# The last layer's expert outputs: added to rows in SBUF by one-hot products on TensorE, instead of accumulated in HBM by indirect DMA

## The chip, the cores and the metric

The kernel runs on one core of a Trainium2 chip. The metric is the device time of one execution in microseconds. The engines are TensorE (PE in the rows, its weight loads PEld), VectorE (DVE), ScalarE (ACT), GpSimd (POOL) and SyncE (SP). A name with q behind it (ACTq, SPq, POOLq) is the part of an engine that issues DMAs. The DMA engines, 16 for the core, carry out what all queues issue.

## The reference

Two layers run over 512 latent tokens and 256 context tokens of width 1024. Each layer has four token mixers, an output projection with a residual, and then expert-choice routing: every one of 16 experts takes the 64 latent tokens (and 32 context tokens, in the first layer only) with the highest scores, runs a SwiGLU network on them, and adds its result to their rows. The last layer's latent rows are the output.

```python
def _ec_ffn(h, w_router, w_gate, w_up, w_down):
    cap = max(1, EC_FACTOR * N // N_EXPERTS)
    aff = jax.nn.softmax((h @ w_router).astype(jnp.float32), axis=-1)
    g, idx = lax.top_k(aff.transpose(0, 2, 1), cap)
    xe = h[bidx, idx]
    hid = (jax.nn.silu(jnp.einsum('becd,edf->becf', xe, w_gate))
           * jnp.einsum('becd,edf->becf', xe, w_up))
    ye = jnp.einsum('becf,efd->becd', hid, w_down) * g[..., None]
    return jnp.zeros_like(h).at[bidx, idx].add(ye)
...
x = x + gt1 * x_mix
h2 = _modulate(_rmsnorm(x, g_ffn[l]), sh2, sc2)
x = x + gt2 * _ec_ffn(h2, w_router[l], w_gate_e[l], w_up_e[l], w_down_e[l])
```

A token may be among the 64 of several experts, or of none; its row then gets several additions, or none.

## The kernel before

Each layer has a stage of mixers (`mixers`), a stage `out_and_route` and a stage `experts`. All matrices are f32.

`out_and_route` finishes the output projection and adds it to the residual rows `x_res` (`resid`, lines 1229 to 1231). `turn` transposes the rows for the router and, once a tile of 128 rows is complete, stores it: in the last layer to `out` itself, on ACT's queue (line 1416). `norm` (lines 1270 to 1274) makes h2, mostly in place, over `x_res`, and ACT's queue stores it to the HBM rows `h2s`. `top` finds the 64 tokens of each expert by eight rounds on VectorE and ends with the indices `idx4` (line 1330), `idx2` (line 1344) and the weights `gval2`.

`experts` then runs expert after expert. POOL gathers the expert's rows of h2 from `h2s` (`gather`, line 1485, an indirect DMA), VectorE transposes them (`turn`, line 1494), TensorE multiplies by w_gate and w_up (`gu`, line 1512, four blocks of weights), ACT and VectorE make `hid` (lines 1521 to 1523), TensorE multiplies by w_down (`down`, line 1545, two blocks), VectorE scales the result to `y_e` (line 1547, 64 tokens in two halves of 512 columns on 128 partitions), and POOL adds it to `out` in HBM by an indirect DMA that accumulates (`add`, line 1526). The half of the partitions with the first 512 columns of the tokens is 0 to 63, the other 64 to 127. TensorE's order is: gate-up blocks A of expert e, w_down of e−1, blocks B of e.

The weights come by SP's queue in loads of 2816 KB, called `w_ex` (`ex_load`, line 1445; the first ones, line 1440, from a copy `w_head` in other order). At most two are in flight (QUEUED = 2). A load's place in SBUF is a block of 22,528 bytes of each partition. A planner (`place`) lays out the whole arena of 183,296 bytes from the life of every tile; beside what else lives in this stage of the last layer, eight blocks fit, and a load waits until the matmuls that read the block's former weights are done. Loads are asked for in the order w_down(e), B(e+1), A(e+2). The planner tries orders of placement drawn from a seed for each part of the program (`SEEDS`), and the schedule of the mixers follows from the plan.

PSUM tiles of the kinds `dn_ps` and `sum_ps` come from one pool (`MM`) of three buffers; the gate-up products use others (`SC`).

Of the kernel before, what the change touches and what calls it, by code (L numbers as in the profile page):

```python
# [17 lines left out]
OP = mybir.AluOpType  # L18
AX = mybir.AxisListType

D = 1024
T = 512
TC = 256
NT = T + TC
L = 2
EPS = 1e-6
E_N = 16
# [26 lines left out]


ARENA = 183296
SEEDS = 48, 0, 1, 0


def lifetimes(instructions, asked):  # L60
# [26 lines left out]
def place_part(lives, room, part, seed, done, tries=400):  # L87

    rnd = random.Random(seed)
    order = sorted(part, key=lambda n: (lives[n][1] - lives[n][0] < 2000, lives[n][0]))  # L90
    for _ in range(tries):
        offs = dict(done)
        for n in order:
            o = fit(lives, room, offs, n)
            if o is None:
                break
            offs[n] = o
        else:
            return offs
        order.remove(n)  # L100
        with_n = [i for i, m in enumerate(order) if m in offs and lives[m][0] <= lives[n][1] and lives[m][1] >= lives[n][0]]
        order.insert(rnd.choice(with_n) if seed and with_n else 0, n)
# [21 lines left out]
class Block:  # L124
# [1043 lines left out]
    def out_and_route(self, l, xs_src, x_dst, ctx_dst):  # L1168
# [9 lines left out]
        next(prelude)  # L1178
        order = cx + lat
        N = len(order)  # L1180
        xr = [self.Q([3, 1024], "x_res") for _ in range(2)]
        rows_x = [xr[n // 3][:, n % 3] for n in range(N)]
        for n, i in enumerate(order):
            self.load_tokens(rows_x[n], xs_src[0 if i < 4 else 1], i, (nc.sync, nc.sync))
        early = [lambda p=p: self.ex_load(l, 0, p, 0) for p in "AAAABBBB"]
        early += [lambda e=e, p=p: self.ex_load(l, e, p, 1) for e, p in HEAD[2:] for _ in range(2)]
        for _ in range((2, 4)[l]):
            early.pop(0)()

# [46 lines left out]
        def turn(n, z):  # L1236
            if z == 0:
                xTs[n] = self.E4([8, 128], "x2T")
            ps = self.MM("x2_tp")
            for k in range(4):  # L1240
                c = 128 * (4 * z + k)
                nc.tensor.transpose(ps[:, 128 * k:128 * k + 128], rows_x[n][:, c:c + 128], self.ident)
            nc.scalar.copy(xTs[n][:, 4 * z:4 * z + 4], ps.rearrange("p (k t) -> p k t", k=4))
            if z:
                i = order[n]
                self.store_tokens(x_dst if i < 4 else ctx_dst, rows_x[n], i, nc.scalar)

# [16 lines left out]
        def norm(n):  # L1264

            i = order[n]
            x, r = rows_x[n], rows[0 if i < 4 else 1]
            h = x if n < N - 2 else self.E4([1024], "h2")
            if n < N - 1:
                nc.vector.scalar_tensor_tensor(h, x, rs[:, i:i + 1], r[:, 2], op0=OP.mult, op1=OP.mult)  # L1270
            else:
                nc.scalar.mul(h, x, rs[:, i:i + 1])
                nc.gpsimd.tensor_mul(h, h, r[:, 2])
            nc.gpsimd.tensor_add(h, h, r[:, 1])
            return lambda *keep: self.store_tokens(self.h2s[0 if i < 4 else 1], h, i, nc.scalar, *keep)
# [2 lines left out]
        self.gval = self.K([3, 16], "gval")  # L1278
        self.idx2 = self.K([16], "idx2", I32)
        self.gval2 = self.K([16], "gval2")  # L1280
        self.groups = [0, 0] + ([] if last else [1])

        def top(m, w):
# [49 lines left out]
            if m == 0:  # L1333
# [8 lines left out]
                nc.vector.tensor_mul(d2[:, 3], d2[:, 3], d2[:, 2])  # L1342
                nc.vector.tensor_add(d2[:, 4], d2[:, 3], d2[:, 0])
                nc.vector.tensor_scalar(self.idx2, d2[:, 4], 0.5, self.misc[:, 6:7], op0=OP.mult, op1=OP.add)
                nc.vector.tensor_tensor(self.gval2, p2[:, 0, 1], d2[:, 1], op=OP.max)

        pick = self.E3([2, 2, 128], "pick", p=64)
# [114 lines left out]
    def experts(self, l, x_rows, tops, tail, early):  # L1462


        nc, io = self.nc, self.io
        G = len(self.groups)
        every = list(range(G))
        hv = [h.rearrange("n (j c) -> (n j) c", j=4) for h in self.h2s]
        xv = [x.rearrange("n (j c) -> (n j) c", j=4) for x in x_rows]
        x2 = x_rows[0].rearrange("n (h c) -> (n h) c", h=2)  # L1470
        wgt = self.wgt

        def load(e, part):
            if e < E_N:
                for _ in range(2 // 1):
                    self.ex_load(l, e, part, 1)

        XG, XT, PG, HID, HT, BK = {}, {}, {}, {}, {}, {}

# [49 lines left out]
        def down(e):  # L1529
# [15 lines left out]
                    nc.tensor.matmul(ps[32 * q:32 * q + 32], HT[e][:, g, k], self.w_dn(e, k, 512 * h, 512 * h + 512),  # L1545
                                     start=(k == 0), stop=(k == 10))
            nc.vector.scalar_tensor_tensor(y[:, 0:512], ps, self.gval2[:, e:e + 1], self.gt2[0], op0=OP.mult, op1=OP.mult)  # L1547
            add(x2, self.idx2[:, e:e + 1], y[:, 0:512])
            del HT[e], HID[e], XT[e], wgt[e]


        if G == 3:
# [16 lines left out]
        gather(1, every)  # L1569
        gu(0, 0, 4, [0, 1])  # L1570
        self.marks.append(len(self.asked))
        load(1, "B")
        gu(0, 4, 8, [0, 1])
        load(2, "A")
        hid(0, [0, 1])
        turn(1, every)
        for e in range(2, 4):
            gather(e, every)
        for e in range(1, E_N):
            gu(e, 0, 4, every)  # L1580
            load(e, "D")
            down(e - 1)
            load(e + 1, "B")
            if e + 1 < E_N:
                turn(e + 1, every)
            gu(e, 4, 8, every)
            load(e + 2, "A")
            hid(e, every)
            if e + 3 < E_N:
                gather(e + 3, every)  # L1590
        down(E_N - 1)

    def run(self):
# [130 lines left out]
def layout(inputs):  # L1724
# [43 lines left out]
    fw = np.zeros((L, 128, 3, 256), np.float32)  # L1768
    fw[:, :, 0], fw[:, 1:, 1], fw[:, ::32, 2] = w[:, 0:128], w[:, :128:-1], w[:, 128:129]
    io["fnet_w"] = fw  # L1770
    io["w_out"] = f("w_out")
    io["w_router"] = f("w_router").reshape(L, 8, 128, 16).transpose(0, 2, 1, 3)

# [44 lines left out]
```

## Time and profile before

| what | value |
| --- | --- |
| three runs | 2737.04, 2738.1, 2740.97 us |
| median | 2738.1 us |
| the profiled execution, its own time | 2742.23 us |
| its span | 2740.4 us |
| granted clock of TensorE, mean over the span | 0.957 |
| TensorE busy | 2429.4 us, 89% |
| VectorE busy | 983.3 us, 36% |
| stage of the mixers, layer 1 | 0 to 985 us, with what stands ahead |
| stages of routing and experts, layer 1 | 985 to 1475 us |
| stage of the mixers, layer 2 | 1475 to 2020 us |
| routing, layer 2 | 2020 to 2092 us |
| experts, layer 2 | 2092 to 2741 us |

The bounds of the stages are read off the timeline and are rough. A row of a window gives the stretch and its length, then the busy time of PE, PEld, DVE, ACT and POOL with the number of instructions, then the granted clock (1.00 is the 2.4 GHz level), the mean busy share of the DMA engines and their GB/s. In a row of a timeline stand the start, the length, the engine and line, the operation with the tiles out<-in, how many instructions the row holds, and in brackets how long the engine was idle ahead of it and what ended that. Two records stand for one f32 matmul. A row of a DMA queue gives packets, MB and the time of its packets as a share of the 16 engines.

### The profile page before, as it was taken

The page shows a single profiled execution, that of the slowest core. Times are in us where ns is not written, and L with a number is a line of the kernel's source. Part 1 is how long each engine was busy: PE and PEld are TensorE (multiplying, and loading weights), DVE is VectorE, ACT ScalarE, POOL GpSimd, SP SyncE. Part 2 cuts the span into 40 slices and gives each one's busy share as a digit, 9 for nine tenths or more (in the row PEclk, how much of TensorE's full clock was granted, in tenths as well). Part 3 has the DMA queues.
Part 4 walks back from the last instruction along what each step waited for, and adds up shares of the span by engine and source line. Part 5 has one row for each costly group of instructions (what it writes and reads, how often), then busy time and mean ns, then how long its engine had stood idle before and what let it go on. Part 6 is the DMA issues. An engine that isn't in the chain of part 4 may idle for free. (4 is left out here: it accounts for less than half of the span.)

```text
span 2740.4 us, 48684 instructions
## 1 busy us (share of the span) xinstructions
PE 2429.4 (89%) x21446; PEld 1679.8 (61%) x21446; DVE 983.3 (36%) x1986; ACT 577.4 (21%) x1094; POOL 474.3 (17%) x347
## 2 busy tenths in 40 slices
PE   7989889999969999999997799999974977777776
PEld 5778889999845555677774677877862422222222
DVE  5666547643251111111112765477432110110101
ACT  4324445433310000000001424344320000000000
POOL 1352332211240111111001211011121111010100
PEclk9999999999989999999998899999996999999999
DMA  7673552323379999999997575544369999999997
GB/s 291 194 246 121 174 167 63 104 82 102 118 301 421 414 415 411 412 414 409 414 413 285 171 233 162 170 127 129 119 208 370 420 419 422 417 419 420 419 418 324
DMA packets 131154, 776.74 MB, mean 283 GB/s; under 512 B 13312, under 2 KB 51072, under 8 KB 107136
## 3 DMA queue, kind: packets, MB, share of 16 engines
q1 hardware_dynamic: 113296, 730.38, 68.5%
q0 software_dynamic: 11776, 25.44, 3.9%
q10 hardware_dynamic: 5872, 17.83, 2.1%
q8 instruction: 168, 2.75, 0.4%
q14 instruction: 42, 0.34, 0.0%
HBM read 734.01 MB, written 39.58 MB: 282 GB/s over the span
## 5 line engine op out<-in xcount | busy, mean ns | idle before, releaser
L1512 PE MATMUL gu_ps<-w_ex,xT 128*32 128x352 f32 x10240 | 815.8, 472 | 131.1 <-DMA w_ex<-in_w_ex 93.7
L1512 PEld LDWEIGHTS gu_ps<-w_ex,xT 128*32 128x32 f32 x10240 | 469.9, 112 | 471.2 <-issue 227.0
L616 PE MATMUL gate_ps<-hh,cw 128*128 128x384 f32 (+1 forms) x1536 | 456.2, 364 | 8.7 <-ACT sg L1010 4.6
L1545 PE MATMUL dn_ps<-w_ex,hidT 128*32 128x512 f32 x2816 | 343.7, 596 | 36.9 <-DMA w_ex<-in_w_ex 34.7
L616 PEld LDWEIGHTS gate_ps<-hh,cw 128*128 128x128 f32 x1536 | 287.5, 192 | 34.3 <-issue 5.4
L1521 ACT ACTIVATE hid<-gu_ps 128x352 f32<-128x352 f32 x80 | 37.1, 464 | 1282.4 <-PE gu_ps L1512 1282.4
L616 PE MATMUL gate_ps<-hl,cw 128*128 128x384 f32 (+1 forms) x768 | 277.8, 362 | 0.0
L1545 PEld LDWEIGHTS dn_ps<-w_ex,hidT 128*32 128x32 f32 x2816 | 115.7, 110 | 232.3 <-issue 192.5
L1547 DVE SCALAR_TENSOR_TENSOR y_e<-dn_ps,gval,gt 128x512 f32<-128x512 f32 x32 | 24.0, 751 | 471.2 <-PE dn_ps L1545 471.2
L1522 DVE TENSOR_TENSOR hid<-hid,gu_ps 128x352 f32<-128x352 f32 x80 | 41.7, 521 | 355.8 <-ACT hid L1521 246.6
L616 PEld LDWEIGHTS gate_ps<-hl,cw 128*128 128x128 f32 x768 | 147.6, 192 | 10.6 <-issue 1.5
L173 DVE TENSOR_TENSOR cw<-craw,cw 128x1280 fp32r<-128x1280 f32 (+1 forms) x72 | 116.8, 1626 | 31.2 <-ACT cw L172 30.8
L1526 POOL DMA_INDIRECT out<-y_e,idx x16 | 25.8, 1609 | 586.4 <-DVE y_e L1547 586.4
L1539 DVE SCALAR_TENSOR_TENSOR y_e<-dn_ps,gval,gt 128x256 f32<-128x256 f32 x16 | 7.7, 484 | 308.9 <-PE dn_ps L1537 308.9
L1030 POOL TENSOR_TENSOR acc<-acc,sg 128x384 f32<-128x384 f32 (+1 forms) x48 | 62.5, 1302 | 321.9 <-DVE sg L1020 223.0
L1526 POOL DMA_INDIRECT cs<-y_e,idx x16 | 27.1, 1691 | 494.0 <-DVE y_e L1539 494.0
L1537 PE MATMUL dn_ps<-w_ex,hidT 128*32 128x256 f32 x1408 | 99.5, 379 | 0.0
L172 ACT CAST cw<-craw 128x1280 fp32r<-128x1280 f32 (+1 forms) x72 | 88.9, 1240 | 38.2 <-PE branch_ps L1014 11.0
L282 POOL TENSOR_TENSOR ada_acc<-ada_acc,w_ada_k 128x1024 f32<-128x1024 f32 x28 | 71.5, 2554 | 130.0 <-ACT w_ada_k L281 129.9
L284 DVE SCALAR_TENSOR_TENSOR ada_acc<-w_ada_k,scT,ada_acc 128x1024 f32<-128x1024 f32 x56 | 81.0, 1446 | 33.0 <-DMA w_ada_k<-in_w_ada 31.2
L1010 ACT ACTIVATE sg<-gate_ps 128x384 f32<-128x384 f32 (+1 forms) x96 | 50.5, 526 | 177.6 <-PE gate_ps L616 148.8
L909 DVE TENSOR_REDUCE df_m<-df_s 128x1 f32<-128x768 f32 (+1 forms) x80 | 66.9, 845 | 34.4 <-PE df_s L908 34.3
(347 smaller groups left out, 3198.2 us busy)
## 6 DMA issues: line engine op xcount, KB each, us to landing
w_ex<-in_w_ex SPq DMA_DIRECT2D x176, 2816.0 KB
w_ada_k<-in_w_ada SPq DMA_DIRECT2D x80, 512.0 KB
craw<-in_w_gb SPq DMA_DIRECT2D x64, 640.0 KB
w_ex<-in_w_head SPq DMA_DIRECT2D x16, 1408.0 KB
w_ex<-in_w_head SPq DMA_DIRECT2D x8, 2816.0 KB
qkv_raws<-in_w_qkv SPq DMA_DIRECT2D x12, 768.0 KB
w_ada<-in_w_ada SPq DMA_DIRECT2D x4, 2048.0 KB
wo_raws<-in_w_out SPq DMA_DIRECT2D x8, 768.0 KB
```

What stands on the lines that cost most here:

```text
L172: self.nc.scalar.copy(hi, src)
L173: self.nc.vector.tensor_sub(lo, src, hi.bitcast(F32))
L282: nc.gpsimd.tensor_add(a, a, t)
L284: nc.vector.scalar_tensor_tensor(a, t, sc, a, op0=OP.mult, op1=OP.add)
L616: nc.tensor.matmul(ps, w[:, lw, k], self.hT(lh, k, t0, t1), start=(k == 0 and s == 0), stop=(k == 7 and s == 2))
L909: nc.vector.tensor_reduce(st[:, m:m + 1], sp[:, 0:n], axis=AX.X, op=OP.max)
L1010: nc.scalar.activation(sg, pg, AF.Tanh, scale=0.5)
L1030: nc.gpsimd.tensor_add(ac, ac, sg)
L1512: nc.tensor.matmul(PG[e, g][s][32 * j:32 * j + 32], XT[e][:, g, c], self.w_gu(e, c, s, j), start=(c == 0), stop=(c == 7))
L1526: nc.gpsimd.indirect_dma_start(out=x, out_offset=bass.IndirectOffsetOnAxis(ap=idx, axis=0), in_=y, in_offset=None, compute_op=OP.add)
L1537: nc.tensor.matmul(ps[32 * j:32 * j + 32], HT[e][:, 2, k], self.w_dn(e, k, 256 * j, 256 * j + 256), start=(k == 0), stop=(k == 10))
L1545: nc.tensor.matmul(ps[32 * q:32 * q + 32], HT[e][:, g, k], self.w_dn(e, k, 512 * h, 512 * h + 512), start=(k == 0), stop=(k == 10))
```

## The change

Only the last layer changes in what it computes where. x is no longer stored to `out` in `out_and_route`; its rows stay in SBUF (`self.X`) through the experts, h2 gets tiles of its own, and the numbers of the tokens (`nat_ids`, one row of 512 on every partition) are loaded beside them. For every expert but the last, `spread` makes a one-hot matrix (which token of the 512 each of the 64 gathered rows is), multiplies it with `y_e` on TensorE, 128 tokens by 512 columns at a time, and VectorE adds the eight products to `self.X`. With the last but one expert's `spread` the finished tiles are stored to `out`, four stores by SP and four by ACT; expert 15's output is still added by the indirect DMA. The weights have seven blocks instead of eight in this stage, one load fewer is asked for ahead of the stage, the loads are asked for through one list (`todo`), and gathers run two experts ahead instead of three. Other seeds for the planner place the tiles of the whole program anew.

```diff
-SEEDS = 48, 0, 1, 0
+SEEDS = 150, 0, 30, 0
...
-        xr = [self.Q([3, 1024], "x_res") for _ in range(2)]
-        rows_x = [xr[n // 3][:, n % 3] for n in range(N)]
+        nx = N // 2
+        xr = [self.Q([nx, 1024], "x_res") for _ in range(2)]
+        rows_x = [xr[n // nx][:, n % nx] for n in range(N)]
+        if last:
+            self.X = rows_x
+            self.nat = self.Q([512], "nat_ids")
+            nc.sync.dma_start(self.nat, io["nat_ids"])
+            h2 = [self.Q([2, 1024], "h2") for _ in range(2)]
...
+        if last:
+            del early[-1]
...
-            if z:
+            if z and not last:
                 i = order[n]
                 self.store_tokens(x_dst if i < 4 else ctx_dst, rows_x[n], i, nc.scalar)
...
-            h = x if n < N - 2 else self.E4([1024], "h2")
+            h = h2[n // 2][:, n % 2] if last else x if n < N - 2 else self.E4([1024], "h2")
...
+                if last:
+                    nc.vector.tensor_scalar(self.tok2, d2[:, 4], 0.25, None, op0=OP.mult)
...
-            add(x2, self.idx2[:, e:e + 1], y[:, 0:512])
+            if last and e < E_N - 1:
+                Y[e] = y
+            else:
+                add(x2, self.idx2[:, e:e + 1], y[:, 0:512])
...
+        def spread(e, then=None):
+            y = Y.pop(e)
+            one = self.E3([512], "onehot")
+            nc.vector.tensor_scalar(one, self.nat, self.tok2[:, e:e + 1], None, op0=OP.is_equal)
+            for i in range(4):
+                for h in range(2):
+                    ps = self.MM("sum_ps")
+                    p = slice(64 * h, 64 * h + 64)
+                    nc.tensor.matmul(ps, one[p, 128 * i:128 * i + 128], y[p, 0:512], start=True, stop=True)
+                    x = self.X[i][:, 512 * h:512 * h + 512]
+                    nc.vector.tensor_add(x, x, ps)
+                if then:
+                    then(i)
...
         for e in range(1, E_N):
             gu(e, 0, 4, every)
-            load(e, "D")
+            load()
             down(e - 1)
-            load(e + 1, "B")
+            load()
             if e + 1 < E_N:
                 turn(e + 1, every)
             gu(e, 4, 8, every)
-            load(e + 2, "A")
+            load()
+            if last and e < E_N - 1:
+                spread(e - 1)
+            elif last:
+                spread(e - 1, lambda i: self.store_tokens(self.out, self.X[i], i, (nc.sync, nc.scalar)[i % 2]))
             hid(e, every)
-            if e + 3 < E_N:
-                gather(e + 3, every)
+            if e + ahead < E_N:
+                gather(e + ahead, every)
         down(E_N - 1)
```

TensorE's order for one expert in the middle of the last stage, before (`gu_ps` are the gate-up products, `dn_ps` the output products, each with the weight block it reads):

```order
L1512 MATMUL gu_ps<-w_ex_18589,xT 32x352 x32
L1512 MATMUL gu_ps<-w_ex_18591,xT 32x352 x32
L1512 MATMUL gu_ps<-w_ex_18660,xT 32x352 x32
L1512 MATMUL gu_ps<-w_ex_18662,xT 32x352 x32
L1545 MATMUL dn_ps<-w_ex_18741,hidT 32x512 x22
L1545 MATMUL dn_ps<-w_ex_18743,hidT 32x512 x22
```

The same place after, from the output blocks of one expert on (`sum_ps` are the products with the one-hot matrix):

```order
L1566 MATMUL dn_ps<-w_ex_18781,hidT 32x512 x22
L1566 MATMUL dn_ps<-w_ex_18830,hidT 32x512 x22
L1586 MATMUL sum_ps<-y_e,onehot 128x512 x3
L1533 MATMUL gu_ps<-w_ex_18832,xT 32x352 x32
L1586 MATMUL sum_ps<-y_e,onehot 128x512 x4
L1533 MATMUL gu_ps<-w_ex_18901,xT 32x352 x32
L1586 MATMUL sum_ps<-y_e,onehot 128x512
L1533 MATMUL gu_ps<-w_ex_18903,xT 32x352 x32
L1533 MATMUL gu_ps<-w_ex_19008,xT 32x352 x32
```

Three sums stand behind the output matmuls, four between the two gate-up blocks that follow, and one behind the second.

VectorE's order for one expert after the change:

```order
L1568 SCALAR_TENSOR_TENSOR y_e<-dn_ps,gval_15903,gt_0_15758 128x512
L1515 STREAM_TRANSPOSE xT<-xg 128x256 x2
L1581 TENSOR_SCALAR onehot<-nat_ids_15685,tok_15904 128x512
L1588 TENSOR_TENSOR x_res_15683<-x_res_15683,sum_ps 128x512 x4
L1588 TENSOR_TENSOR x_res_15684<-x_res_15684,sum_ps 128x512 x4
L1543 TENSOR_TENSOR hid<-hid,gu_ps 128x352
L1544 STREAM_TRANSPOSE hidT<-hid 128x352
```

The one-hot product and the eight additions have come between the two transposes of the gathered rows and the multiply of `hid`, which were neighbours before.

ACT's order at the end of the routing stage, before (the stores to `out` carry x, those to `h2s` carry h2):

```order
L1416 DMA out<-x_res_15682 8x8x1024 x2
L1416 DMA h2s_15893<-x_res_15682 8x8x1024 x2
L1260 ACTIVATE aff,rt_m<-aff,rt_m 128x16
L1243 COPY x2T<-x_tp 128x512
L1231 ACTIVATE res_t,ffn_ss<-x_res_15683 128x512
L1243 COPY x2T<-x_tp 128x512
L1416 DMA out<-x_res_15683 8x8x1024 x2
L1260 ACTIVATE aff,rt_m<-aff,rt_m 128x16
L1272 ACTIVATE h_16187<-x_res_15683,ffn_rs 128x1024
L1416 DMA h2s_15893<-x_res_15682 8x8x1024 x2
L1416 DMA h2s_15893<-h_16168 8x8x1024 x2
L1416 DMA h2s_15893<-h_16187 8x8x1024 x2
```

And after:

```order
L1428 DMA h2s_15898<-h_327_15687 8x8x1024 x2
L1269 ACTIVATE aff,rt_m<-aff,rt_m 128x16
L1252 COPY x2T<-x_tp 128x512
L1240 ACTIVATE res_t,ffn_ss<-x_res_15684 128x512
L1252 COPY x2T<-x_tp 128x512
L1269 ACTIVATE aff,rt_m<-aff,rt_m 128x16
L1281 ACTIVATE h_328_15688<-x_res_15684,ffn_rs 128x1024
L1428 DMA h2s_15898<-h_327_15687 8x8x1024 x2
L1428 DMA h2s_15898<-h_328_15688 8x8x1024 x4
```

The stores of x are gone from this queue, here and (two pairs) ahead of it; the eight of h2 stand where they stood.

## Rows read from the trace of the kernel before

**Rows 1.** Windows: stretch, length, busy us by engine, clock, DMA share, GB/s.

```profile
2020.00:2092.00 72.00, 35.01 (x215) 29.84 (x217) 31.30 (x94) 12.62 (x30) 26.10 (x18) 0.73 0.74 280
...
2200.00:2727.00 527.00, 398.94 (x4232) 148.20 (x4234) 55.48 (x86) 12.04 (x26) 36.79 (x30) 0.95 1.00 417
```

**Rows 2.** Timeline of TensorE, stage of the experts, layer 2.

```profile
2091.80 22.07 PE L1512 MATMUL gu_ps<-w_ex,xT 128*32 128x352 f32 x256 [20.89 <-issue]
...
2164.41 19.28 PE L1512 MATMUL gu_ps<-w_ex,xT 128*32 128x352 f32 x256
2183.51 9.84 PE L1545 MATMUL dn_ps<-w_ex,hidT 128*32 128x512 f32 x88
...
2373.23 6.63 PE L1512 MATMUL gu_ps<-w_ex,xT 128*32 128x352 f32 x64 [2.02 <-DMA w_ex<-in_w_ex]
```

**Rows 3.** Timeline of VectorE in the same stage.

```profile
2136.13 0.75 DVE L1547 SCALAR_TENSOR_TENSOR y_e<-dn_ps,gval,gt 128x512 f32<-128x512 f32 x1 [19.32 <-PE dn_ps L1545]
...
2164.66 0.75 DVE L1547 SCALAR_TENSOR_TENSOR y_e<-dn_ps,gval,gt 128x512 f32<-128x512 f32 x1 [17.20 <-PE dn_ps L1545]
...
2193.40 0.75 DVE L1547 SCALAR_TENSOR_TENSOR y_e<-dn_ps,gval,gt 128x512 f32<-128x512 f32 x1 [17.40 <-PE dn_ps L1545]
2194.07 1.15 DVE L1494 STREAM_TRANSPOSE xT<-xg 128x256 f32<-128x256 f32 x2
...
2237.09 0.75 DVE L1547 SCALAR_TENSOR_TENSOR y_e<-dn_ps,gval,gt 128x512 f32<-128x512 f32 x1 [25.39 <-PE dn_ps L1545]
...
2703.68 0.75 DVE L1547 SCALAR_TENSOR_TENSOR y_e<-dn_ps,gval,gt 128x512 f32<-128x512 f32 x1 [24.57 <-PE dn_ps L1545]
...
2733.17 0.75 DVE L1547 SCALAR_TENSOR_TENSOR y_e<-dn_ps,gval,gt 128x512 f32<-128x512 f32 x1 [12.73 <-PE dn_ps L1545]
```

**Rows 4.** Page, DMA issues of the whole program.

```profile
w_ex<-in_w_ex SPq DMA_DIRECT2D x176, 2816.0 KB
```

**Rows 5.** Timeline of SyncE's queue, 2095 to 2102 us.

```profile
2099.72 0.34 SPq L1445 DMA_DIRECT2D w_ex<-in_w_ex  x1
```

**Rows 6.** Timeline of all engines, the end of the span.

```profile
2721.20 11.93 PE L1545 MATMUL dn_ps<-w_ex,hidT 128*32 128x512 f32 x88 [2.67 <-DMA w_ex<-in_w_ex]
...
2727.78 4.01 PEld L1545 LDWEIGHTS dn_ps<-w_ex,hidT 128*32 128x32 f32 x42 [0.45 <-DMA w_ex<-in_w_ex]
...
2734.20 1.55 POOL L1526 DMA_INDIRECT out<-y_e,idx  x1 [27.76 <-DVE y_e L1547]
```

**Rows 7.** DMA queues, 2662 to 2682 us, with one accumulate.

```profile
q0 software_dynamic: 144, 0.26, 7.2%
```

**Rows 8.** DMA queues, 2680 to 2703 us, with no accumulate.

```profile
q1 hardware_dynamic: 496, 9.89, 100.1%
```

**Rows 9.** Timeline of TensorE, pooling mixer of layer 2.

```profile
1660.85 1.88 PE L687 MATMUL poolw_ps<-icd,pool_w 128*128 128x512 f32 x4
```

**Rows 10.** Groups by line and shape, VectorE: busy us, mean ns.

```profile
L1522 DVE TENSOR_TENSOR hid<-hid,gu_ps 128x352 f32<-128x352 f32 x80 | 41.7, 521 | 355.8 <-ACT hid L1521 246.6 <-PE gu_ps L1512 109.1
...
L811 DVE TENSOR_SCALAR na_p<-na_p,na_m 128x512 f32<-128x512 f32 x32 | 17.6, 552 | 0.7
...
L1230 DVE TENSOR_TENSOR x_res<-x_res,res_t 128x512 f32<-128x512 f32 x10 | 6.9, 692 | 0.3
```

**Rows 11.** Timeline of all engines, routing of layer 2.

```profile
2050.34 1.89 ACTq L1416 DMA_DIRECT2D out<-x_res  x2
...
2052.91 0.59 ACTq L1416 DMA_DIRECT2D h2s<-x_res  x1
...
2058.79 5.45 ACTq L1416 DMA_DIRECT2D h2s<-h  x4
...
2070.90 0.25 DVE L1330 SCALAR_TENSOR_TENSOR idx<-topk,misc 128x32 int32<-128x32 f32 x1
...
2083.18 1.09 POOL L1485 DMA_INDIRECT xg<-h2s,idx  x1 [24.09 <-DMA h2s<-h]
```

**Rows 12.** DMA queues, 2060 to 2070 us (q10 is ACT's).

```profile
q10 hardware_dynamic: 230, 0.84, 20.5%
```

More of the change, by code (lines that the diff above doesn't have):

```diff
@@ L89, in place_part @@
     rnd = random.Random(seed)
-    order = sorted(part, key=lambda n: (lives[n][1] - lives[n][0] < 2000, lives[n][0]))
+    order = sorted(part, key=lambda n: (seed % 2 == 0 and lives[n][1] - lives[n][0] < 2000, lives[n][0]))
     for _ in range(tries):
@@ L1280, in out_and_route @@
         self.gval2 = self.K([16], "gval2")
+        self.tok2 = self.K([16], "tok2")
         self.groups = [0, 0] + ([] if last else [1])
@@ L1466, in experts @@
         G = len(self.groups)
+        last = l == L - 1
         every = list(range(G))
@@ L1471, in experts, with load @@
         wgt = self.wgt
[L1473 to L1476, printed above, removed]
+        todo = [(1, "B"), (2, "A")]
+        for e in range(1, E_N):
+            todo += [(e, "D"), (e + 1, "B"), (e + 2, "A")]
+        todo = [p for p in todo if p[0] < E_N for _ in range(2)]
+        if last:
+            todo.insert(0, (0, "D"))
+        def load(n=2):
+            for _ in range(n):
+                if todo:
+                    self.ex_load(l, *todo.pop(0), 1)
         XG, XT, PG, HID, HT, BK = {}, {}, {}, {}, {}, {}
@@ L1547, in down @@
             nc.vector.scalar_tensor_tensor(y[:, 0:512], ps, self.gval2[:, e:e + 1], self.gt2[0], op0=OP.mult, op1=OP.mult)
-            add(x2, self.idx2[:, e:e + 1], y[:, 0:512])
+            if last and e < E_N - 1:
+                Y[e] = y
+            else:
+                add(x2, self.idx2[:, e:e + 1], y[:, 0:512])
             del HT[e], HID[e], XT[e], wgt[e]
+        Y = {}
+        def spread(e, then=None):
[11 more added lines that the diff above has]
+                    then(i)
         if G == 3:
@@ L1571, in experts @@
         self.marks.append(len(self.asked))
-        load(1, "B")
+        load()
         gu(0, 4, 8, [0, 1])
-        load(2, "A")
+        load()
         hid(0, [0, 1])
         turn(1, every)
-        for e in range(2, 4):
+        ahead = 2 if last else 3
+        for e in range(2, ahead + 1):
             gather(e, every)
@@ L1580, in experts @@
             gu(e, 0, 4, every)
-            load(e, "D")
+            load()
             down(e - 1)
-            load(e + 1, "B")
+            load()
             if e + 1 < E_N:
@@ L1586, in experts @@
             gu(e, 4, 8, every)
-            load(e + 2, "A")
+            load()
+            if last and e < E_N - 1:
+                spread(e - 1)
+            elif last:
+                spread(e - 1, lambda i: self.store_tokens(self.out, self.X[i], i, (nc.sync, nc.scalar)[i % 2]))
             hid(e, every)
-            if e + 3 < E_N:
-                gather(e + 3, every)
+            if e + ahead < E_N:
+                gather(e + ahead, every)
         down(E_N - 1)
@@ L1770, in layout @@
     io["fnet_w"] = fw
+    io["nat_ids"] = np.broadcast_to(nat.astype(np.float32), (128, T))
     io["w_out"] = f("w_out")
```

## The prediction, made before the changed kernel had run

> **What bounds the kernel now.** I read the windows first, one per stage of the second layer. The experts stage fills the end of the span, 2092 to 2741 us. In its long middle part the DMA engines show a share of 1.00 at 417 GB/s while TensorE (PE) is busy 398.94 of 527.00 us; the reader is to see that the pace there is that of the transfers [rows 1]. The stage ahead of it, 2020 to 2092 us, is the loosest: DMA share 0.74, PE busy 35.01 of 72.00 us [rows 1]. The timeline of TensorE agrees. From 2164.41 us one expert's 256 gate-up records and 88 output records run without a gap; later each block of weights is waited for, as in the row at 2373.23 us, 2.02 us idle that ended with a transfer of `w_ex` [rows 2]. VectorE's (DVE) product `y_e` stands once per expert and is the clock of the stage: 28.74 us from 2164.66 to 2193.40 us at TensorE's full pace, and (2703.68 − 2237.09) / 11 = 42.42 us once the eight blocks fetched ahead are used up [rows 3]. So two prices per expert compete: TensorE needs 28.7 us, the transfers 42.4 us. The kernel pays the second.
>
> **What the transfers cost, and what the change takes off them.** Each layer has 88 loads of `w_ex` [rows 4]; here the first is issued at 2099.72 us [rows 5], and the last half of expert 15's w_down is waited for at 2727.78 us [rows 6], 628.1 us later. In 20 us with one accumulate, that accumulate's queue takes 7.2% of all DMA engines, 1.44 us [rows 7]; with none, the loads alone fill 100.1% [rows 8]. The change replaces 15 of the stage's 16 accumulates; 14 of them lie ahead of the last load, 14 × 1.44 = 20.2 us. Without them a block takes (628.1 − 20.2) / 88 = 6.91 us, six of them 41.4 us per expert (gathers included). On the other side the residual stream x (16,384 B of each partition) and the token numbers `nat_ids` (2,048 B) now stay in SBUF, and the room for weights falls from eight blocks to seven: one block more is loaded inside the stage, 6.9 us. Net for the transfers alone: −13 us.
>
> **What the change puts on TensorE and VectorE.** Per expert: one one-hot product on VectorE, eight f32 matmuls of 64 rows into 128x512, and eight additions. The matmul with the nearest row is `poolw`, four records in 1.88 us, 0.43 us from start to start [rows 9]; an f32 matmul leaves two records (256 gate-up records of an expert [rows 2] for the 128 instructions in the order), so 0.86 us each and 6.9 us for eight. The one-hot product is nearest to a 128x512 TENSOR_SCALAR at 0.55 us, an addition to `x_res` at 0.69 us [rows 10]. None of it lies beside other work by itself, since the order on each engine is fixed:
> - TensorE runs the first three sums right behind expert e−1's output matmuls. They need `y_e` (0.75 us), and in VectorE's order two transposes (1.15 us for both [rows 3]) and the one-hot product (0.55 us) come first. TensorE stands still for 2.5 us with the hops. The gate-up matmuls that stand behind the sums wait too.
> - The last sum stands behind the last gate-up block. VectorE does its addition (0.69 us) before the multiply of `hid` (0.52 us [rows 10]), and only this frees the PSUM into which the next expert's first gate-up matmul writes: 1.6 us with hops.
> - The other adds run beside gate-up blocks of some 4.8 us; three PSUM buffers are enough for that.
>
> So TensorE's own pace becomes 28.74 + 2.5 + 6.9 + 1.6 + 0.3 (estimate for drains between the kinds of matmul) = 40.0 us. That is just under 41.4 us, the pace of the transfers. The bounds: 37.4 us if neighbouring sums, which read different halves of the rows, run two at once (one pair among the first three, two among the next four, 0.86 us saved by each), and 46 us if each of the eight sums waited for the addition before it (0.69 us and a hop).
>
> The Trainium skill (TensorEngine Tiling (Array Packing), Tiling Modes, Key Properties) says that tiles on different rows run their matmuls independently, and that a switch of the tiling mode drains the engine. By it the eight sums, which alternate between rows 0–63 and 64–127, would take four times 0.86 us, 3.4 us, the period of TensorE would be 36.6 us, and the loads would stay the bound at 41.4. The trace of before has no such pair; what it has is four column tiles at once, 88 output records of 0.6 us in 9.84 us. That is why I keep the concurrent case as a rival and not as my value.
>
> **What the change takes off the stage ahead.** Before, ACT's queue stores x to `out` (eight stores of 256 KB), and the h2 rows follow on the same queue: the last two x stores are issued at 2050.34 us, the last h2 rows at 2058.79 us [rows 11]. The queue moves 0.84 MB in 10 us, a share of 20.5% beside the weight loads [rows 12]. The indices are written by 2071.2 us, but POOL's first gather starts at 2083.18 us, idle for the 24.09 us before, and what ended that was the store of h2 [rows 11]. Without the x stores only h2 is on the queue: its last six stores, 1.57 MB, from 2052.91 us on, take 18.7 us at 0.084 MB/us and land at 2071.6. So the gather starts at about 2072 us, held by the indices and the stores alike. From the gather to the first gate-up matmul it is 2091.80 − 2083.18 = 8.6 us [rows 2, 11], so this one starts at about **2081 us**, 11 us earlier. Bounds: 0 (something else holds the gather) and 11.7 us (the indices alone hold it, 2071.5). h2's own tiles now hold the room of one head load until h2 is stored; that load is one of the last three ahead of the stage, and it has until its expert is due, some 40 us later. The new product `tok2` (0.2 us on VectorE, behind the indices) and the load of `nat_ids` lie under that wait; gathers are fetched two experts ahead instead of three, still 80 us ahead of their use.
>
> **The sum, paced by TensorE.** First gate-up at 2081; the first `y_e` comes 2136.13 − 2091.80 = 44.3 us later [rows 2, 3], 2125.3; 14 periods of 40.0 us give 2685.3 for expert 14's `y_e`. Then the last expert: 2.5 + eight sums 6.9 + two gate-up blocks 9.6 (half of 19.28) = 19.0; the wait for `hid` 2.7 and 88 output records, some 9.9 [rows 2, 6]; and from the last `y_e` at 2733.17 us to the end of the span at 2740.4 us 7.3 us for the accumulate that stays [rows 3, 6]. Together 38.9: the span ends at 2724.2 us. The transfers don't stop this: the first load in the stage moves with the first gate-up to 2088.9 us, and 89 blocks of 6.91 us end at 2703.9 us, when TensorE has still to sum and multiply gate-up. The eight stores of x to `out` (2 MB, about 5 us of transfers) run during the last gate-up and output matmuls; uncovered they would cost up to 5 us, since the last accumulate waits for all eight. The profiled execution took 2742.2 us for a span of 2740.4; 2724.2 + 1.8 = 2726.0, 16.2 us under it. Against the median of 2738.1 us, 4.1 us below the profiled one, that is **2722 us**.
>
> **The rivals.**
> - *Two sums run at once; the loads stay the bound* (37.4 us per expert). TensorE alone would end at about 2685 us; the last block lands at 2703.9, its output half takes 4.9 and the end 7.3 us: a span of 2716, or 2721 with the stores of `out` uncovered: 2714 to 2719 us. For it: four column tiles do run at once in the output matmuls. Against it: every sum has an addition behind it on VectorE. Chance 0.25.
> - *The gather is not earlier*, since h2's stores still land at 2083 beside the weight loads: TensorE's sum moves by 11 us, 2733 us. For it: the queue's 20.5% share is what it gets while the loads run. Against it: 2 MB less stand ahead. Chance 0.13.
> - *TensorE becomes the bound with more than 41.15 us per expert*, **slower** than before. Each microsecond on the period costs 14; with 16.2 / 14 = 1.15 us more than my 40.0 the gain is gone. The place: sums four to seven, with three PSUM buffers that the output matmuls share; where each sum waits for the addition before it (0.69 us and a hop, four times) the period is 43.0 us and the time 2722 + 14 × 3.0 = 2764. For it: VectorE's order has four additions in a row before anything else. Against it: the buffers are freed while a gate-up block runs. Chance 0.12.
> - *The rest of the program takes it back.* The new seeds lay out SBUF anew and shift the order in both layers' mixers. Nothing in the trace prices this; I allow 10 us either way, so up to no change at all (2732 to 2738). Chance 0.10.
>
> **How the numbers follow.** Main case 0.40, own range 2714 to 2730. With the loads-bound rival it lies on the faster side, 0.65; with most of the late gather (2733 is 0.19% under the median, so just about no change: half of it) and half of the reshuffle it is 0.76. A difference of 0.2%, 5.5 us, is about what a measurement of this kernel can tell. No change 0.10, slower 0.14 (the TensorE rival and a little of the reshuffle). The range 2708 to 2741 leaves out the slower rival and the far ends of the reshuffle.
>
> **What would show it.** Right: POOL's first gather at about 2072 us and the first gate-up at 2081; `y_e` every 40 us; idle time of TensorE ahead of the sums ended by VectorE and not by transfers; a DMA share under 1.00 in the stage; sums 0.86 us apart. Sums half as far apart, with waits for `w_ex` still there, speak for the first rival; a period above 41.15 us with waits on additions speaks for the third; a first layer that ends earlier or later than before speaks for the fourth.

## The result, and the profile after

The changed kernel took 2711.85 us (median of 4 runs, 2708.14 to 2715.49) against 2739.53 us of the kernel before on the same chip: a ratio of 0.9897, interval 0.9878 to 0.9915, some 28 us faster. Forecast were 2722 us and a range of 2708 to 2741. The profiled execution took 2712.24 us, its span 2710.5, 29.9 us under the span before.

The windows of the kernel after (stretch, length, busy us by engine, clock, DMA share, GB/s) answer to [rows 1]:

```profile
2020.00:2092.00 72.00, 41.01 (x386) 26.73 (x384) 26.57 (x85) 8.74 (x20) 24.14 (x16) 0.74 0.78 301
...
2200.00:2690.00 490.00, 442.82 (x4387) 158.40 (x4386) 119.64 (x195) 11.60 (x26) 18.90 (x20) 0.98 1.00 425
```

TensorE is now busy 442.82 of 490 us, and yet the DMA share is still 1.00: both are close to full.

VectorE's timeline after, the answer to [rows 3]:

```profile
2114.68 0.75 DVE L1568 SCALAR_TENSOR_TENSOR y_e<-dn_ps,gval,gt 128x512 f32<-128x512 f32 x1 [20.95 <-PE dn_ps L1566]
...
2188.19 0.75 DVE L1568 SCALAR_TENSOR_TENSOR y_e<-dn_ps,gval,gt 128x512 f32<-128x512 f32 x1 [17.20 <-PE dn_ps L1566]
2226.61 0.75 DVE L1568 SCALAR_TENSOR_TENSOR y_e<-dn_ps,gval,gt 128x512 f32<-128x512 f32 x1 [17.20 <-PE dn_ps L1566]
2266.68 0.75 DVE L1568 SCALAR_TENSOR_TENSOR y_e<-dn_ps,gval,gt 128x512 f32<-128x512 f32 x1 [17.19 <-PE dn_ps L1566]
...
2631.46 0.75 DVE L1568 SCALAR_TENSOR_TENSOR y_e<-dn_ps,gval,gt 128x512 f32<-128x512 f32 x1 [18.98 <-PE dn_ps L1566]
2672.99 0.75 DVE L1568 SCALAR_TENSOR_TENSOR y_e<-dn_ps,gval,gt 128x512 f32<-128x512 f32 x1 [20.31 <-PE dn_ps L1566]
2701.60 0.75 DVE L1568 SCALAR_TENSOR_TENSOR y_e<-dn_ps,gval,gt 128x512 f32<-128x512 f32 x1 [9.77 <-PE dn_ps L1566]
```

The period is 38.42 or 40.07 us early, 41.53 us late. TensorE's timeline of one expert, and three rows from later, the answer to [rows 2]:

```profile
2190.42 1.98 PE L1586 MATMUL sum_ps<-y_e,onehot 64*128 64x512 f32 x6 [2.30 <-DVE onehot L1581]
2192.33 4.94 PE L1533 MATMUL gu_ps<-w_ex,xT 128*32 128x352 f32 x64
2197.20 3.03 PE L1586 MATMUL sum_ps<-y_e,onehot 64*128 64x512 f32 x8
2200.16 4.94 PE L1533 MATMUL gu_ps<-w_ex,xT 128*32 128x352 f32 x64
2205.03 1.12 PE L1586 MATMUL sum_ps<-y_e,onehot 64*128 64x512 f32 x2
2207.36 9.74 PE L1533 MATMUL gu_ps<-w_ex,xT 128*32 128x352 f32 x128 [1.21 <-DVE hid L1543]
2216.92 9.62 PE L1566 MATMUL dn_ps<-w_ex,hidT 128*32 128x512 f32 x88
2228.84 2.30 PE L1586 MATMUL sum_ps<-y_e,onehot 64*128 64x512 f32 x6 [2.30 <-DVE onehot L1581]
2231.07 6.26 PE L1533 MATMUL gu_ps<-w_ex,xT 128*32 128x352 f32 x64
...
2420.43 5.34 PE L1566 MATMUL dn_ps<-w_ex,hidT 128*32 128x512 f32 x44 [1.11 <-DMA w_ex<-in_w_ex]
```

The waits stand where the order put them: 2.30 us for the one-hot matrix, 1.21 us for `hid`. Three sums take 1.98 us and four 3.03, less than 0.86 us each. From 2420 us on TensorE waits for weights again, seven times and 6.1 us in all, where it was 128.4 us before. The routing stage after, the answer to [rows 11]:

```profile
2038.42 6.89 ACTq L1428 DMA_DIRECT2D h2s<-h  x5
...
2055.37 0.25 DVE L1340 SCALAR_TENSOR_TENSOR idx<-topk,misc 128x32 int32<-128x32 f32 x1
...
2061.21 1.09 POOL L1506 DMA_INDIRECT xg<-h2s,idx  x1 [17.16 <-DMA h2s<-h]
```

The gather starts 5.6 us behind the indices instead of 12.0 us. But the indices themselves are written 15.5 us earlier, which the forecast's sum did not have. SP's queue issues the 88 loads from 2081.37 on, here with the same row of before:

```profile
2081.37 599.99 SPq L1457 DMA_DIRECT2D w_ex<-in_w_ex  x88
2681.41 14.61 SPq L1428 DMA_DIRECT2D out<-x_res  x4
```

```profile
2099.72 614.21 SPq L1445 DMA_DIRECT2D w_ex<-in_w_ex  x88
```

So the 29.9 us of the span fall into six pieces that follow one another: indices −15.5; from the indices to the gather −6.4 (12.0 to 5.6); from there to the first gate-up matmul +0.2 (8.62 to 8.79); to the first of the 88 loads +3.4 (7.92 to 11.37); from the first to the last load issued −14.2 (614.21 to 599.99); from there to the end of the span +2.6 (26.5 to 29.1).

### The profile page after: what moved, and what is told of

Its sections match the earlier page's. It is cut to its first block, busy times and chain, and to the rows that moved or that the text cites. A ratio compares the mean times of both kernels' runs of the same rounds, so it can differ in the third digit from the quotient of the medians.

```text
span 2710.5 us, 49269 instructions
## 1 busy us (share of the span) xinstructions
PE 2488.2 (92%) x21686; PEld 1690.5 (62%) x21686; DVE 1058.2 (39%) x2122; ACT 576.2 (21%) x1094; POOL 444.7 (16%) x332
## 4 chain that ended last, share of the span: by engine, by line
PE 46%; DMA 24%; issue 12%; DVE 5%; POOL 1%; ACT 1%; SPq 0%; POOLq 0%; ACTq 0%; DVEq 0%
PE gate_ps L616 14%; DMA w_ex<-in_w_ex 13%; PE gu_ps L1533 11%; PE dn_ps L1566 4%; DMA cs<-y_e,idx 4%; PE branch_ps L1014 3%; PE wo_ps L1392 2%; DMA w_ex<-in_w_head 2%; DMA w_ada_k<-in_w_ada 1%; PE sum_ps L1586 1%; DMA h2s<-h 1%; PE df_o L947 1%; PE dn_ps L1558 1%; DMA out<-x_res 1%; DVE ada_acc L284 1%
## 5 line engine op out<-in xcount | busy, mean ns | idle before, releaser
L1533 PE MATMUL gu_ps<-w_ex,xT 128*32 128x352 f32 x10240 | 800.1, 466 | 48.3 <-DVE xT L1515 30.7
L1533 PEld LDWEIGHTS gu_ps<-w_ex,xT 128*32 128x32 f32 x10240 | 459.0, 111 | 388.4 <-issue 234.4
L1566 PE MATMUL dn_ps<-w_ex,hidT 128*32 128x512 f32 x2816 | 334.1, 592 | 10.0 <-DMA w_ex<-in_w_ex 6.1
L1506 POOL DMA_INDIRECT xg<-h2s,idx x64 | 62.0, 969 | 525.4 <-PE gu_ps L1533 470.9
L1588 DVE TENSOR_TENSOR x_res<-x_res,sum_ps 128x512 f32<-128x512 f32 x120 | 77.2, 684 | 173.7 <-PE sum_ps L1586 173.4
L1586 PE MATMUL sum_ps<-y_e,onehot 64*128 64x512 f32 x240 | 94.6, 654 | 31.1 <-DVE onehot L1581 31.1
```

What stands on the lines that cost most here:

```text
L1506: ins = nc.gpsimd.indirect_dma_start(out=XG[e][:, g], out_offset=None, in_=hv[m], in_offset=bass.IndirectOffsetOnAxis(ap=self.idx4[:, g, e ...
L1533: nc.tensor.matmul(PG[e, g][s][32 * j:32 * j + 32], XT[e][:, g, c], self.w_gu(e, c, s, j), start=(c == 0), stop=(c == 7))
L1586: nc.tensor.matmul(ps, one[p, 128 * i:128 * i + 128], y[p, 0:512], start=True, stop=True)
L1588: nc.vector.tensor_add(x, x, ps)
```

## The experiments

Three theories were to be told apart: the loads set the pace to the end (so that the sums cost almost nothing); TensorE sets it (the forecast's main case); the new plan of the tiles does most. The table gives the pieces of each run's profile in us (indices written; indices to gather; loads issued from first to last; last load issued to end of span) and the measured ratio to the kernel before.

| run | indices | to gather | loads | end | ratio, interval |
| --- | --- | --- | --- | --- | --- |
| before | 2071.2 | 12.0 | 614.2 | 26.5 | 1 |
| after | 2055.6 | 5.6 | 600.0 | 29.1 | 0.9897 (0.9878 to 0.9915) |
| after again (e10) | 2048.8 | 5.0 | 600.3 | 28.6 | 0.9882 (0.9863 to 0.9901) |
| before, new seeds (e2) | 2057.3 | 10.5 | 615.4 | 26.4 | 0.9963 (0.9949 to 0.9977) |
| before, third plan (e13) | 2055.2 | 5.8 | 613.8 | 34.1 | 0.9968 (0.9956 to 0.9980) |
| x stored too (e3) | 2049.3 | 11.2 | 600.1 | 29.5 | 0.9908 (0.9889 to 0.9927) |
| adds back (e7) | 2052.3 | 11.4 | 617.5 | 26.7 | 0.9946 (0.9928 to 0.9964) |
| one sum of eight (e4) | 2042.7 | 6.8 | 599.4 | 26.0 | 0.9862 (0.9840 to 0.9885) |
| sums by half (e5) | 2047.3 | 5.3 | 599.9 | 49.1 | 0.9954 (0.9938 to 0.9971) |
| before, no adds (e6) | 2065.7 | 10.9 | 598.8 | 25.9 | 0.9932 (0.9914 to 0.9950) |
| h2 on two queues (e9) | 2055.1 | 3.1 | 599.5 | 30.2 | 0.9862 (0.9830 to 0.9894) |
| the same again (e11) | 2047.3 | 2.8 | 599.9 | 30.0 | 0.9876 (0.9854 to 0.9897) |
| two adds (e12) | 2052.3 | 4.8 | 614.7 | 25.9 | 0.9924 (0.9903 to 0.9944) |
| two adds, ACT stores (e14) | 2055.9 | 4.6 | 608.4 | 27.3 | 0.9909 (0.9891 to 0.9927) |

The third row warns of the first column: the same kernel wrote its indices at 2055.6 in one profile and at 2048.8 in another (its variants between 2042.7 and 2055.9), while its loads agree within 0.4 us. One profile of each kernel prices the piece of the loads well, and the program ahead of the stage only to some 7 us or worse; there the ratios decide.

**The plan alone (e2), and another plan (e13).**

```diff
-SEEDS = 48, 0, 1, 0
+SEEDS = 150, 0, 30, 0
```

> The kernel before with the planner's seeds of the changed kernel (150, 0, 30, 0) and nothing else. Theory: the indices of the last layer come 15.5 us earlier in the changed kernel (2055.5 against 2071.2 us) because the other plan takes waits out of the second layer's mixers; then they come at about 2056 us here too and the time is 2739.5 - 15 = 2724 us (2720 to 2729). Rival: the mixers ended earlier because of the tiles and the stores that the change takes out of the last layer, and the seeds do nothing by themselves: indices at 2071 us, 2735 to 2743 us.

> The kernel before with a third plan (seeds 150, 0, 8, 0). Theory: what the seeds give is a draw; the indices of the last layer come somewhere between 2050 and 2075 us, the loads take 614 to 617 us, and the time follows the indices one to one. Rival: the indices come at 2057 us as with the seeds of the change, and the old plan was an unusually slow one.

With the seeds alone the indices come at 2057.3 us, and the ratio of 0.9963 makes it some 10 us, not 15. The third plan (150, 0, 8, 0) has them at 2055.2 us and gains 9 us (its profile has an end longer by 7.6 us, at a granted clock of 0.941 over the run, which was not followed up). Both drawn plans beat the old one, so that the old one looks like the slow one, as the rival said; two draws can't show how they spread. TensorE's waits in the second layer's mixers, 1490 to 2040 us (what waited, what for, us in all, times, longest), before:

```profile
PE wo_ps L1380 <- ACT wo_w L172: 9.1, 1, 9.1
...
PE na_s L796 <- DMA na_head<-na_st: 4.5, 2, 3.7
...
PE df_s L907 <- DMA df_head<-df_st: 4.1, 1, 4.1
PE df_s L907 <- ACT df_p L912: 4.0, 4, 2.4
```

and with the new seeds alone:

```profile
PE wo_ps L1380 <- ACT wo_w L172: 5.5, 1, 5.5
...
PE df_s L907 <- ACT df_p L912: 2.9, 3, 2.1
PE na_s L796 <- DMA na_head<-na_st: 2.1, 1, 2.1
...
PE df_s L907 <- DMA df_head<-df_st: 0.8, 1, 0.8
```

These four waits fall from 21.7 to 11.3 us, all of TensorE's waits in the stretch from 60.2 to 47.0. That is of the size of the ratio's 10 us; which of the waits are on the path was not traced.

**x stored to `out` ahead (e3), and the adds by DMA as well (e7).**

```diff
-            if z and not last:
+            if z:
```

In e7, beside this:

```diff
-            else:
-                add(x2, self.idx2[:, e:e + 1], y[:, 0:512])
+            add(x2, self.idx2[:, e:e + 1], y[:, 0:512])
...
-                for h in range(2):
+                for h in range(1 - i % 2):
...
-                spread(e - 1, lambda i: self.store_tokens(self.out, self.X[i], i, (nc.sync, nc.scalar)[i % 2]))
+                spread(e - 1)
```

> The changed kernel with the eight stores of x to out on ACT's queue put back (they are overwritten at the end). Theory: the h2 stores land later, the first gather comes 12 us behind the indices as before instead of 5.7, the weights start some 6 us later, and since they bind to the end the time is 2711.9 + 6 = 2718 us (2715 to 2722). Rival: these stores are hidden, because the indices or the head loads hold the gather: 2709 to 2714 us.

> The changed kernel with x stored to out ahead (as in the run before) and all 16 outputs added to out by the indirect DMA again; two sums of eight are left in so that x keeps its place in SBUF, and the stores of x at the end are gone. Seven blocks, the new plan. Theory: 6 us for the x stores and 14 x 1.44 = 20 us for the adds come back, and the end is some 4 us shorter: 2711.9 + 22 = 2734 us (2729 to 2738), with y_e every 42 us. Rival: TensorE with its sums sets the pace of the changed kernel, so that taking six sums away gives back most of what the adds cost: 2718 to 2726 us.

With the x stores back the gather is 11.2 us behind the indices again, so they were what held it, with the plan of the change; the time grows by 3 us (0.9908 against 0.9897), or by 7 us beside the second measurement of the change (0.9882), where that piece grows by 5.6 to 6.2 us; the intervals overlap. In the third plan the gather waits only 5.8 us although x is stored, so the price hangs on the plan; why was not traced. With the adds back the 88 loads take 617.5 us, 17.4 more than in e3. Its span is 17.2 us over the change's: 17.5 more for the loads, 5.8 for the gather, 2.4 less at the end, and indices that came 3.3 us sooner. By the ratios it is 13 us (0.0049), under the 17 to 26 us of the theory and within the rival's 6 to 14; beside the second measurement of the change it is 18 us. So the time doesn't decide. What decides against the rival is the piece of the loads, and e4 below.

**The adds left out of the kernel before (e6; 15 experts' outputs are missing).**

```diff
-            add(x2, self.idx2[:, e:e + 1], y[:, 0:512])
+            if l < L - 1 or e == E_N - 1:
+                add(x2, self.idx2[:, e:e + 1], y[:, 0:512])
```

> The kernel before with the accumulates of the first 15 experts of the last layer left out (their outputs are missing). Theory: the 88 loads of the last stage are issued over 600 us instead of 614, as in the changed kernel, and the time falls by 14 to 17 us, to a ratio of 0.994 to 0.995. Rival: the accumulates cost the loads the 1.44 us of all engines that their queue takes, 20 us: ratio 0.9927 or less. Other rival: they fill gaps of the loads and cost nothing: ratio 0.998 to 1.000.

The loads go from 614.2 to 598.8 us, 15.4. The ratio gives 18.6 us, 13.7 to 23.6; it can't decide between 15 and 20, the loads can. The adds' price is 14 to 17 us, and it shows in the time.

**One sum of eight (e4; most of 15 experts' outputs is missing).** In `spread` seven of the eight matmuls and additions are left out.

```diff
-                for h in range(2):
+                for h in range(1 if i == 0 else 0):
                     ps = self.MM("sum_ps")
```

> The changed kernel with one of the eight sums of each expert (the other seven and their additions are left out, so 15 experts' outputs are mostly missing). Theory: the loads bind; the first experts run at 32 us each, then TensorE waits for w_ex, y_e comes every 41.4 us, the last weights land at about 2690 us as in the changed kernel, and only the end is shorter, by the six or seven sums and waits of the last expert: 2702 to 2708 us. Rival: TensorE at 40.5 us per expert is the bound of the changed kernel: without the sums the last weights land 10 us earlier or more, 2685 to 2698 us.

The loads take 599.4 us, as with all sums, and from 2247.11 to 2661.00 us `y_e` comes every 41.4 us, ten times. From expert 0's `y_e` to expert 14's it is 557.7 us, and 558.3 with all sums. So TensorE's 6 us of sums per expert are free there, and the loads bind in the changed kernel up to expert 14's output. That is against the forecast's main case. The transfers themselves set the pace of the loads: from 2100 to 2690 us of the changed kernel SP's loads wait 552.9 us for earlier loads and 0.5 us for TensorE. In the stage only the end is shorter, by 3.1 us, and part of that can come from the stores of x: six of the eight go out in the routing stage in this kernel, since nothing is added to their rows any more. By the ratios the run is 5 to 10 us faster than the change. Its indices came at 2042.7 us, the earliest of all; why was not traced.

**Sums by half (e5).** The loops over `h` and `i` change places, so that neighbours read the same rows.

```diff
-            for i in range(4):
-                for h in range(2):
+            for h in range(2):
+                for i in range(4):
...
-                if then:
-                    then(i)
+                    if then and h:
+                        then(i)
```

> The changed kernel with the eight sums of an expert in another order: first the four that read rows 0 to 63, then the four that read rows 64 to 127, so that neighbours read the same rows. Theory: in the changed kernel neighbours on different rows overlap (three sums in 1.98 us, four in 3.03, where 0.86 each would be 2.6 and 3.4); here the groups of three and four take 2.6 and 3.4 us, the first experts 39.0 us instead of 38.4, and since the loads bind the time grows by about 1 us at the end: 2711 to 2715 us. Rival: the short groups have another cause (a part of each product is skipped or not recorded) and stay 1.98 and 3.03 us.

```profile
2233.01 2.95 PE L1586 MATMUL sum_ps<-y_e,onehot 64*128 64x512 f32 x6 [2.30 <-DVE onehot L1581]
2235.89 6.46 PE L1533 MATMUL gu_ps<-w_ex,xT 128*32 128x352 f32 x64
2242.28 3.02 PE L1586 MATMUL sum_ps<-y_e,onehot 64*128 64x512 f32 x8
...
2355.76 2.84 PE L1586 MATMUL sum_ps<-y_e,onehot 64*128 64x512 f32 x6 [2.30 <-DVE onehot L1581]
2358.53 4.94 PE L1533 MATMUL gu_ps<-w_ex,xT 128*32 128x352 f32 x64
2363.40 3.02 PE L1586 MATMUL sum_ps<-y_e,onehot 64*128 64x512 f32 x8
```

In the first expert shown the gate-up block takes 6.46 us, at a lowered clock; in the second it takes 4.94 us, as in the changed kernel. There three sums take 2.84 us instead of 1.98, so neighbours on different rows did overlap. The group of four takes 3.02 us in both orders. In the changed kernel its four alternate between the halves and could overlap twice. What holds them there are the additions, 0.65 us apart with three PSUM buffers between: of the last group of four in the changed kernel the fourth weight load waits 0.75 us for one.

```profile
2674.19 3.03 PE L1586 MATMUL sum_ps<-y_e,onehot 64*128 64x512 f32 x8 [1.25 <-DVE onehot L1581]
...
2675.35 2.59 DVE L1588 TENSOR_TENSOR x_res<-x_res,sum_ps 128x512 f32<-128x512 f32 x4 [1.22 <-PE sum_ps L1586]
2676.09 0.29 PEld L1586 LDWEIGHTS sum_ps<-y_e,onehot 64*128 64x128 f32 x2 [0.75 <-DVE x_res L1588]
```

That agrees with the Trainium skill (TensorEngine Tiling (Array Packing), PSUM Bottleneck): tiling speeds TensorE up but not the emptying of PSUM.

The time was misjudged: not 1 us but some 16 us more than the change's. The overlap costs what was expected, 39.28 us per expert against 38.42 where the clock stays at 1.00. What the expectation left out is the clock, which falls further here than in the changed kernel. Windows of two experts that follow one another (stretch, length, busy us by engine, clock, DMA share, GB/s):

```profile
2188.16:2230.78 42.62, 39.10 (x360) 13.79 (x360) 9.97 (x17) 0.93 (x2) 1.90 (x2) 0.92 1.00 427
2230.78:2271.69 40.91, 37.41 (x360) 13.36 (x360) 9.97 (x16) 0.93 (x2) 1.89 (x2) 0.96 1.00 426
```

On the mean TensorE takes (2681.14 − 2188.16) / 12 = 41.1 us per expert. The loads are still issued over 599.9 us, but expert 14's `y_e` comes 8.4 us after the last load was issued (2681.14 against 2672.75), where in the changed kernel it comes 8.4 us ahead of it (2672.99 against 2681.36). TensorE never waits for weights in this stage now: it has become the bound, and the changed kernel stands right beside that edge.

**h2 on two queues (e9, e11).** Half of each h2 tile is stored by POOL's queue.

> The changed kernel with the h2 stores of the last layer over two queues, half of each tile by ACT and half by POOL. Theory: the first gather stands 5.6 us behind the indices because the h2 stores on one queue get a fifth of the DMA engines beside the loads; over two queues they land some 6 us earlier, the gather follows the indices within 2 us, the loads start 4 to 6 us earlier and the time is 2706 to 2708 us. Rival: POOL is late with its half since it computes h2 itself, or the stores share the same engines: 2710 us or more.

> The kernel with the h2 stores over ACT and POOL once more, to compare with the changed kernel on one chip. Theory: its gather follows the indices 2 us sooner, so its ratio is lower by 0.001 (2 to 3 us). Rival from the first medians: lower by 0.003 or more. Other rival: no difference, the interval of both holds the same values.

The gather follows the indices after 3.1 and 2.8 us instead of 5.6 and 5.0, not within 2 as the theory had it. Beside the changed kernel on one chip the ratios are 0.9876 and 0.9882: the 2 us that the profile shows are there or not, the intervals can't tell. Of the kernels that compute everything it has the lowest median, but it is not shown to beat the change.

**Two adds at the end (e12, e14).** Expert 14 is added by DMA too, and x is stored one expert earlier, by SP and ACT (e12) or by ACT alone (e14).

```diff
-            if last and e < E_N - 1:
+            if last and e < E_N - 2:
                 Y[e] = y
...
-            elif last:
+            elif last and e == E_N - 2:
```

> The changed kernel with expert 14's output added by the indirect DMA too, so that the last sums and the stores of x stand one expert earlier. Theory: the loads bind to the end; the 2 MB of stores and one more accumulate lie between the last loads, and leaving the sums out behind expert 14 gives nothing: the time is that of the changed kernel within 3 us, the sum of the end (last load issued to end of span) 24 to 27 us instead of 29, and the loads 603 to 606 us instead of 600. Rival: the last sums on TensorE hold the end: 5 to 8 us faster, with the loads still at 600 us.

> The changed kernel with expert 14's output added by the indirect DMA too, and all eight stores of x on ACT's queue, so that SP's last load of weights no longer stands behind stores. Theory: the loads bind to the end and the stores and the second accumulate take their share of the DMA engines from the last loads: the last load lands some 6 us later, TensorE waits for it, and the ratio is that of the changed kernel, 0.987 to 0.991. Rival: the sums behind expert 14's output hold the end, and leaving them out gives 5 to 8 us: ratio 0.985 to 0.987. If it is as slow as the run with stores on SP (0.9924), that slowness was not the load behind the stores.

```profile
2673.46 3.00 SPq L1428 DMA_DIRECT2D out<-x_res  x4
2691.68 0.33 SPq L1457 DMA_DIRECT2D w_ex<-in_w_ex  x1
```

In e12 SP's last load stands behind stores of x on its queue and waits 13.8 us for one of them to land. TensorE then waits for the load, as its timeline shows:

```profile
2701.92 8.29 PE L1566 MATMUL dn_ps<-w_ex,hidT 128*32 128x512 f32 x44 [8.06 <-DMA w_ex<-in_w_ex]
```

That makes the run 7 to 12 us slower than the change, by a wait that the expectation had not seen. With ACT's queue alone the load isn't held, but the loads still take 608.4 us, 8.4 more, for an end that is 1.8 us shorter; its ratio and that of e12 can't be told apart. Leaving out the last sums gives nothing that the loads don't take back: in both runs TensorE waits for `w_ex` up to the last block. The changed kernel is another case at its very end. Its last wait for weights ends at 2667.60 us, and what follows is its own chain of sums, products and the accumulate, 43 us:

```profile
2667.60 5.34 PE L1566 MATMUL dn_ps<-w_ex,hidT 128*32 128x512 f32 x44 [1.26 <-DMA w_ex<-in_w_ex]
...
2691.88 9.65 PE L1566 MATMUL dn_ps<-w_ex,hidT 128*32 128x512 f32 x88 [1.97 <-DVE hidT L1544]
```

## Why the prediction was right, and where it was not

- **The bound.** The main case, that TensorE paces the stage, failed in the step "That is just under 41.4 us, the pace of the transfers" and in "The transfers don't stop this". TensorE takes 28.74 + 2.30 + 1.98 + 3.03 + 1.12 + 1.21 = 38.4 us, not 40.0. The sums are 6.1 us and not 6.9, since one pair of the first three overlaps; the waits are 2.30 for 2.5 and 1.21 for 1.6; for the 0.3 of drains no room is left in the measured 38.42. With every second expert at 40.07 us this is a mean of 39.2 us. At that pace TensorE uses up the blocks fetched ahead by 2420 us, and from then on the period is that of the loads, 41.3 us on the mean (2383.61 to 2672.99). The rival on concurrent sums had the mechanism. What the Trainium skill (TensorEngine Tiling (Array Packing), Key Properties) says of tiles on different rows is borne out for one pair of the first three sums, not for four pairs.
- **The sum from the first gate-up on.** It comes out nearly as forecast, and that is luck: 640.5 us to the end of the span (2070.00 to 2710.5) for 643.2, and 558.3 / 14 = 39.9 us per period for 40.0. That figure is the mean of 38.4 us over the first seven periods, where TensorE sets the pace (the first of them only 35.3), and of 41.3 over the last seven, where the loads do; with one sum of eight (e4) it is 39.8. Of the 13.7 us by which the span was missed, 11.0 lie ahead of the first gate-up, which came at 2070.0 and not at 2081.
- **The adds.** Mis-sized: 20.2 us were forecast from the share of their queue, 14.2 us came off the loads (15.4 and 17.4 in the two experiments). Why the share of the queue says too much was not tried.
- **The lost block.** 6.9 us were forecast. The extra load is one from `w_head`, issued at 2076.64 us between the first gate-up matmul and the first of the 88 loads, and that piece grew by 3.4 us. Whether this is its price stays open: the third plan, with eight blocks, has 11.85 us there as well.
- **The gather.** The mechanism was right (e3), the size not: 11 us forecast, 6.4 us measured. The h2 stores still hold it for 5.6 us after the indices.
- **The plan.** The step "Nothing in the trace prices this" left it at zero in the sum, with 10 us either way and a chance of 0.10 for the loss alone. The seeds alone gave 10 us (e2), and in the pair of profiles the indices come 15.5 us earlier, the largest piece. How much of the other 5 us is the draw of an execution and how much is that the change's own tiles make another plan stays open, since the old seeds leave no room for the changed kernel's last stage. The profiles speak for the second: from the last output matmul of layer 1 to the indices it is 583.5 and 577.2 us with the old plan (before, e6), 573.8 with the new seeds alone (e2), but 559.5 to 567.3 in the ten profiles of the changed kernel and its variants.
- **The end.** 7.3 us from the last `y_e` were forecast; 2710.5 − 2701.60 = 8.9 us came. POOL's timeline has the accumulate 1.65 us behind the end of `y_e`. With the stores of x one expert earlier (e12, the second row, and e14) it is 0.3 us, so what it waits for are these stores:

```profile
2704.00 1.63 POOL L1547 DMA_INDIRECT out<-y_e,idx  x1 [134.47 <-issue]
...
2711.30 1.57 POOL L1547 DMA_INDIRECT out<-y_e,idx  x1 [17.09 <-DVE y_e L1568]
```

So the pieces behind the indices make −6.4 + 0.2 + 3.4 − 14.2 + 2.6 = −14.4 us, close to the 16 forecast by another route, and what came earlier ahead of them adds the rest. That the time lies in the range of 2708 to 2741 is owed in part to errors that cancel; it lies outside the main case's own 2714 to 2730, and outside the 2714 to 2719 of the rival whose mechanism held.

## What to carry to other kernels

A change that needs other seeds, other tiles or another order is two changes: run the kernel before with the new plan alone, or its gain will be put down to the idea. Where two resources need 39 and 41 us for the same step, ask of every edit which of the two it touches: here sums were free as long as TensorE stayed below the loads, and changing two loops over was enough to make the kernel 16 us slower. Split a span at the events that each piece hangs on (indices, gather, first load, last load, end), and compare pieces: from the indices on they repeated to some half a microsecond in two profiles of the changed kernel, where the whole spans differ by eight.

## What the runs showed of the hardware that was not expected

TensorE's granted clock falls for a few microseconds after its waits, but not with every expert: from 2188 to 2384 us with every second one, later with some and not with others. Windows of the changed kernel (as above): one expert, the next one, and within it the stretch after the wait:

```profile
2188.20:2226.60 38.40, 34.91 (x360) 12.71 (x360) 9.77 (x16) 0.93 (x2) 1.89 (x2) 1.00 1.00 427
2226.60:2266.70 40.10, 36.56 (x360) 12.92 (x360) 9.82 (x17) 0.93 (x2) 1.89 (x2) 0.96 1.01 426
...
2231.10:2237.30 6.20, 6.20 (x67) 2.20 (x66) 0.79 (x2) 0.00 (x0) 0.00 (x0) 0.78 1.01 428
```

Both experts wait the same 2.30 us for the one-hot matrix. In the second the clock is 0.78 over 6.2 us, a mix of the levels of 2.4 and 1.2 GHz; the sums take 2.30 instead of 1.98 us, the gate-up block 6.26 instead of 4.94, and the expert 1.65 us more. Why it falls with one expert and not with the next was not tried.
